# Two layers of a hybrid decoder trunk on one core: sixteen of the twenty-two gate/up tiles of each layer as seven half products, with the weight sums on VectorE

## The chip, the core and the metric

The kernel runs on one core of a Trainium2 chip. The metric is device time in microseconds (us), the median of three runs of the whole program; smaller is better. The core has TensorE (PE in the profile, its weight loads apart as PEld), VectorE (DVE), ScalarE (ACT), GpSimd (POOL) and SyncE (SP), which issues nearly all DMAs here.

## The reference

A trunk of two layers over 512 tokens of width 1024. Each layer mixes tokens (three groups of heads behind one input projection, then an output projection) and then runs a SwiGLU feed-forward of width 2816, each between RMS norms and with a residual. The change is in the feed-forward:

```python
def hybrid_layer(x, ...):
    h = rms_norm(x, pre_mix_norm)
    proj = h @ w_in
    ...
    mix = jnp.concatenate([y_ssd, y_sb, y_moba], axis=-1) @ w_out
    x = x + rms_norm(mix, post_mix_norm)
    h2 = rms_norm(x, pre_ffn_norm)
    f = (jax.nn.silu(h2 @ w_gate) * (h2 @ w_up)) @ w_down
    return x + rms_norm(f, post_ffn_norm)
```

All tensors are float32. The kernel keeps every matrix product at nearly that precision by splitting both operands into a high and a low part of the type fp32r, which TensorE takes, and adding three products (high by high, high by low, low by high).

## The kernel before

One function, `trunk`, writes the whole program; a scheduler then sets the order of the instructions of each engine from the order in which they are written, from priorities (`tc.high_priority(offset=...)`) and from its own estimate of when operands are ready. Each engine then runs its instructions strictly in that order, and waits on semaphores where an operand or a buffer isn't ready.

Weights come in chunks of 128 partitions by 1024 numbers (512 KB). `chunk` (L120) takes one of three raw buffers `wr`, starts the DMA on SP's queue (L122), and splits the chunk into `wh` and `wl`, four buffers of each: ScalarE rounds into `wh` (`split`, L108), and VectorE subtracts that from the raw chunk into `wl` (L109). A raw buffer is free for the next DMA once L109 has read it; a pair `wh`, `wl` is free once TensorE has used it.

The feed-forward's input `h2` stands transposed (features on partitions, tokens along the free dimension) in two tiles `hT`, the high and the low part, eight blocks of 128 features by 512 tokens. `pre_norm` (L173) makes it, token tile by token tile (four tiles of 128 tokens): normalize (L179), transpose on TensorE into a PSUM bank (`to_fm`, L164), split from the bank into `hT` (`to_hT`, L108 and L109). For token tiles 2 and 3 it has one bank each, so that the second four of eight transposes wait until the first four have been split.

Gate and up (L580 to L590): 22 feature tiles `i`. Each takes a gate chunk and an up chunk and runs 24 matmuls for each of them (8 blocks of features by three passes; `fm_mm`, L206, matmul at L210), every one with a 128x128 stationary block of weights and 512 tokens moving, into a bank of PSUM each. The first two tiles (`CUT = 2`) run as two halves of 256 tokens, so that the first half can start before token tiles 2 and 3 are there. Then `silu` of the gate bank on ScalarE (L147) and the product with the up bank on VectorE (L590) give `GT[i]`. There are four pairs of banks in turn.

Down (L596 to L619): for each `i`, `GT[i]` is split into `gs`, two of eight tiles `R` (L606), and TensorE multiplies it with a down chunk (L599), 24 matmuls of 512 columns into all eight banks. In the mixer the tiles `R` serve the softplus values of one attention and the output projection's left operand; the tiles `F28` to `F39` hold the mixer's outputs and scratch.

The lines that the change and the prediction touch: `to_hT` (L167), `pre_norm` (L173), the tile lists (L66, L67, L82, L226), the gate/up loop (L577 to L590), the row loads of the gains behind it (L592 to L594), and the first splits of the down loop (L606).

## Time and profile before

| | us |
|---|---|
| median of three runs (1266.46 to 1266.77) | 1266.76 |
| the profiled execution's own time | 1262.44 |
| its span, first to last instruction | 1260.6 |
| PE busy in it | 1235.3 |
| DVE busy | 612.5 |
| ACT busy | 498.6 |
| one whole gate/up tile of 512 tokens (48 matmuls), from the trace | 10.88 |

TensorE is busy for 98% of the span, at full clock nearly throughout; VectorE and ScalarE are busy for half of it or less. The gate/up stage is about 283 to 511 us in the first layer and 905 to 1134 us in the second, the down stage about 116 us behind each. A busy share says only how long an instruction occupied its engine; how fast instructions follow each other is read from their start times in the timeline.

### The profile page before, as it was taken

What the parts mean: (1) busy time and instruction counts of PE and PEld (TensorE: products, weight loads), DVE (VectorE), ACT (ScalarE), POOL (GpSimd) and SP (SyncE); (2) the same over time, 40 slices, a digit from 0 to 9 for tenths busy, and PEclk for the clock granted to TensorE, in tenths of its full rate; (3) what the DMA queues carried; (4) which work ended last, traced back from release to release, by engine and by line L of the source; (5) the groups of instructions that cost most, each with busy time, mean ns of one, the idle gap of its engine ahead of it and who ended that gap; (6) DMA issues with size and microseconds to landing.
All of it is one profiled execution on the core that took longest, in us unless ns stands there. A gap on an engine that the chain in (4) does not pass through costs nothing.

```text
span 1260.6 us, 15385 instructions
## 1 busy us (share of the span) xinstructions
PE 1235.3 (98%) x6118; PEld 1037.5 (82%) x6118; DVE 612.5 (49%) x1011; ACT 498.6 (40%) x892; POOL 53.8 (4%) x88
## 2 busy tenths in 40 slices
PE   6999999999999999999999999999999999999997
PEld 5787888898888888888877788888988888888886
DVE  5466857874322222333465577588542222223334
ACT  5556763453222222332355656536432222222332
POOL 1010000100000000000010100001000000000000
PEclk9999999999999999999999999999999999999999
DMA  6332223343233332233333322133242322332321
GB/s 241 118 108 77 85 93 101 109 134 113 89 99 101 100 95 91 100 100 100 101 109 108 134 69 84 60 100 117 93 134 100 98 90 97 101 101 96 90 83 67
DMA packets 40760, 128.70 MB, mean 102 GB/s; under 512 B 5456, under 2 KB 5744, under 8 KB 40688
## 3 DMA queue, kind: packets, MB, share of 16 engines
q1 hardware_dynamic: 39344, 123.49, 30.5%
q0 software_dynamic: 1344, 4.23, 1.0%
q8 instruction: 48, 0.79, 0.3%
q14 instruction: 24, 0.20, 0.0%
HBM read 123.47 MB, written 4.23 MB: 101 GB/s over the span
## 4 chain that ended last, share of the span: by engine, by line
PE 95%; DVE 2%; ACT 1%; issue 1%; DMA 0%; SPq 0%; DVEq 0%; POOLq 0%; POOL 0%; ACTq 0%
PE B L210 52%; PE B L599 18%; PE B L201 7%; PE B L549 7%; PE B L324 2%; PE B L331 1%; PE B L437 1%; PE B L302 1%; PE B L164 1%; PE B L509 1%; PE B L303 1%; PE B L433 1%; PE B L351 1%; PE B L560 0%; PE B L515 0%
## 5 line engine op out<-in xcount | busy, mean ns | idle before, releaser
L210 PE MATMUL B<-hT,wh 128*128 128x512 f32 (+1 forms) x2048 | 609.0, 379 | 2.2 <-ACT F L291 2.2
L210 PEld LDWEIGHTS B<-hT,wh 128*128 128x128 f32 x2048 | 376.1, 189 | 71.6 <-ACT F L291 3.3
L210 PE MATMUL B<-hT,wl 128*128 128x512 f32 (+1 forms) x1024 | 386.6, 378 | 0.0
L109 DVE TENSOR_TENSOR wl<-wr,wh 128x1024 fp32r<-128x1024 f32 x204 | 248.6, 1224 | 254.1 <-ACT wh L108 252.6
L108 ACT ACTIVATE wh<-wr 128x1024 fp32r<-128x1024 f32 x204 | 214.9, 1057 | 391.3 <-PE B L210 314.1
L210 PEld LDWEIGHTS B<-hT,wl 128*128 128x128 f32 x1024 | 193.3, 189 | 33.7
L599 PE MATMUL B<-wh,R 128*128 128x512 f32 x704 | 190.1, 389 | 0.0
L599 PEld LDWEIGHTS B<-wh,R 128*128 128x128 f32 x704 | 132.1, 188 | 27.4
L599 PE MATMUL B<-wl,R 128*128 128x512 f32 x352 | 110.0, 389 | 0.0
L109 DVE TENSOR_TENSOR R<-F,R 128x512 fp32r<-128x512 f32 (+2 forms) x76 | 45.9, 607 | 122.1 <-ACT R L108 121.9
L108 ACT ACTIVATE R<-F 128x512 fp32r<-128x512 f32 (+2 forms) x76 | 42.4, 560 | 144.1 <-PE B L599 139.0
L590 DVE TENSOR_TENSOR F<-B,F 128x512 f32<-128x512 f32 x44 | 30.4, 691 | 127.6 <-PE B L210 127.6
L201 PE MATMUL B<-wh,hT 128*128 128x512 f32 x256 | 82.7, 399 | 2.4 <-DVE hT L109 2.4
L599 PEld LDWEIGHTS B<-wl,R 128*128 128x128 f32 x352 | 66.1, 188 | 13.7
L549 PE MATMUL B<-wh,R 128*128 128x512 f32 x256 | 76.9, 398 | 0.0
L155 POOL TENSOR_TENSOR SM<-SM,mhalf 128x1 f32<-128x1 f32 (+2 forms) x50 | 35.4, 711 | 737.1 <-DVE SM L154 464.5
L201 PEld LDWEIGHTS B<-wh,hT 128*128 128x128 f32 x256 | 48.0, 190 | 12.9 <-DVE hT L109 2.9
L549 PEld LDWEIGHTS B<-wh,R 128*128 128x128 f32 x256 | 47.6, 188 | 9.9 <-DVE R L109 0.4
L201 PE MATMUL B<-wl,hT 128*128 128x512 f32 x128 | 50.5, 394 | 0.0
L143 ACT ACTIVATE F<-F 128x512 f32<-128x512 f32 (+3 forms) x80 | 39.0, 499 | 16.2 <-DVE F L220 15.2
L549 PE MATMUL B<-wl,R 128*128 128x512 f32 x128 | 43.0, 394 | 0.0
L464 DVE SCALAR_TENSOR_TENSOR F<-B,cw,F 128x511 f32<-128x511 f32 (+2 forms) x48 | 35.7, 745 | 10.4 <-ACT F L462 9.9
(147 smaller groups left out, 990.8 us busy)
## 6 DMA issues: line engine op xcount, KB each, us to landing
wr<-in_wch_dram SPq DMA_DIRECT2D x204, 512.0 KB, 3.6
x<-in_x_dram SPq DMA_DIRECT2D x16, 256.0 KB, 3.6
F<-in_gains_dram SPq DMA_DIRECT2D x16, 256.0 KB, 4.7
F<-acd POOLq DMA_DIRECT2D x16, 256.0 KB, 6.2
xsave<-x SPq DMA_DIRECT2D x8, 256.0 KB, 2.1
x<-xsave SPq DMA_DIRECT2D x8, 256.0 KB, 3.4
out_dram<-x SPq DMA_DIRECT2D x8, 256.0 KB, 2.1
F<-in_mixgain_dram SPq DMA_DIRECT2D x4, 256.0 KB, 4.9
```

What stands on the lines that cost most here:

```text
L108: A.activation(hi, src, AF.Copy)
L109: return eng.tensor_tensor(lo, src, hi.bitcast(F32), op=OP.subtract)
L143: order["exp"][group] = A.activation(o, i, f, **kw)
L155: G.tensor_tensor(r, m, mhalf[:, 0:n], op=OP.pow)
L164: T.transpose(p[:, i * P:(i + 1) * P], srcs[q + i], ident)
L201: T.matmul(p, hT[a][:, k, t * P:(t + 1) * P], w[k // 2][b][:, (k % 2) * 512:(k % 2 + 1) * 512], start=n == 0, stop=n == 3 * KT - 1)
L210: T.matmul(p[:, t0 * P:t1 * P], w[b][:, k * P:(k + 1) * P], hT[a][:, k, t0 * P:t1 * P], start=first and n == 0, stop=n == 3 * KT - 1, skip ...
L324: T.matmul(pz[:, o:w], ntri if i2 == i else nones, s2, start=False, stop=i2 == NT - 1 and n == 1, skip_group_check=True)
L464: V.scalar_tensor_tensor(u[:, j:], p[:, :S - j], cw[:, i, 3 - j:4 - j], u[:, j:], op0=OP.mult, op1=OP.add)
L549: T.matmul(OB[j][hf], lt, w[b][:, hf * 512:(hf + 1) * 512], start=k == ks[0] and a == 0 and b == 0, stop=k == ks[-1] and a == 1)
L590: V.tensor_tensor(GT[i], pu, sg, op=OP.mult)
L599: T.matmul(B[2 * t + hf], gs[a][:, t * P:(t + 1) * P], w[b][:, hf * 512:(hf + 1) * 512], start=i == 0 and a == 0 and b == 0, stop=i == HT ...
```

## The change

The gate/up product of a tile is seen as a 2 by 2 block product. Let `A` be the input, cut in token halves (rows) and feature halves (columns), and `B` the gate and up weights of a feature tile, cut in feature halves (rows) with gate and up as its two columns. The eight half products (12 matmuls of 256 columns each, with the three passes) are replaced for 16 of the 22 tiles by seven, in Winograd's form of Strassen's scheme. Tiles 0, 1, 5, 9, 13 and 17 stay as they were (`PLAIN`).

Three things are added for that:

- sums of the input, once in a layer: `pre_norm` also copies the transposed, unsplit input to spare tiles (`keep`, on ScalarE), and VectorE forms four combinations of each feature-half block (eight subtractions or sums of 128x512) and splits them into `XS` (eight more operations of 128x512 on VectorE, eight on ScalarE);
- sums of the weights, for each of the 16 tiles: four sums of 128x512 on VectorE, and the split of them and of two raw blocks: `w0` (gate, 1024), `t24` (two blocks of 512, split apart), `t13` (1024), `b22` (512). One tile takes all four pairs of `wh` and `wl`, and both its raw chunks must be there for the first sum;
- the outputs are put together from four half banks with seven operations of 128x256 on VectorE, one copy and two `silu` of 128x256 on ScalarE.

A tile's matmuls have 256 columns: 84 of them instead of 48 of 512. The eight half banks of two sets take turns. To make room, the tiles `R` become halves of four tiles `RR`, and `F28` to `F39` halves of six tiles `D`; in the gate/up stage `D0` to `D5`, `RR0` and `RR1` hold `XS`, and `RR2` and `RR3` the weight sums. The down stage takes `RR` back.

```diff
+PLAIN = (0, 1, 5, 9, 13, 17)
...
-    def to_hT(t):
+    def to_hT(t, keep=None):
         def dst(q, n, p):
+            if keep is not None:
+                A.activation(keep[q // 4], p, AF.Copy)
             sl = slice(t * P, (t + 1) * P)
             split(p.rearrange("p (k l) -> p k l", k=4), hT[0][:, q:q + n, sl], hT[1][:, q:q + n, sl])
...
+        QA = [[QF[0], F[22]], [QF[1], F[23]], [F[24], F[26]], [F[25], F[27]]]
...
-                    pre_norm(j, grow2, take_jk(), ring(OB[j] if j < 2 else OB[j][0:1]))
+                    pre_norm(j, grow2, take_jk(), ring(OB[j] if j < 2 else OB[j][0:1]), QA[j])
...
+        k4 = "p (k l) -> p k l"
+        XS = [slot(f"D{i}", F32R, D) for i in range(6)] + RR[0:2]
+        XS = [[t.rearrange(k4, k=4) for t in XS[2 * i:2 * i + 2]] for i in range(4)]
+        TT = [slot(f"RR{i}", F32, D) for i in (2, 3)]
+        for c in range(2):
+            (a11, a12), (a21, a22) = QA[c], QA[2 + c]
+            s2, s3 = QF[4 + c], QF[2 + c]
+            V.tensor_tensor(a22, a22, a21, op=OP.subtract)
+            V.tensor_tensor(s2, a11, a22, op=OP.add)
+            V.tensor_tensor(s3, a11, a21, op=OP.subtract)
+            V.tensor_tensor(a12, s2, a12, op=OP.subtract)
+            for n, src in enumerate((a22, s2, s3, a12)):
+                split(src.rearrange(k4, k=4), *[x[:, :, c * P:(c + 1) * P] for x in XS[n]])
...
+        def left(j, a, k):
+            if j < 3:
+                return hT[a][:, k + (4 if j else 0), 256 if j == 2 else 0:512 if j == 2 else 256]
+            return XS[j - 3][a][:, k]
+
+        def product(p, w, half, j, first):
+            for k in range(4):
+                for n, (a, b) in enumerate(PASSES):
+                    T.matmul(p, w[b][:, half * 512 + k * P:half * 512 + (k + 1) * P], left(j, a, k),
+                             start=first and k == 0 and n == 0, stop=k == 3 and n == 2, skip_group_check=True)
+
+        def plain(i):
             wg = chunk(l, C_GU + 2 * i)
             wu = chunk(l, C_GU + 2 * i + 1)
...
+        def seven(i):
+
+            rg, ru = take_raw(), take_raw()
+            b11, b21, b12, b22 = rg[:, lo5], rg[:, hi5], ru[:, lo5], ru[:, hi5]
+            for n, r in enumerate((rg, ru)):
+                nc.sync.dma_start(r, wch[l, C_GU + 2 * i + n])
+            t13, t24 = TT
+            w0, w24, w13, w22 = [(take_hi(), take_lo()) for _ in range(4)]
+            with tc.high_priority(offset=SPLIT_OFF):
+                split(rg, *w0)
+                V.tensor_tensor(t13[:, lo5], b11, b12, op=OP.add)
+                V.tensor_tensor(t24[:, lo5], t13[:, lo5], b22, op=OP.add)
+                split(t24[:, lo5], w24[0][:, lo5], w24[1][:, lo5])
+                V.tensor_tensor(t13[:, hi5], b12, b22, op=OP.add)
+                split(t13, *w13)
+                V.tensor_tensor(t24[:, hi5], t24[:, lo5], b21, op=OP.add)
+                split(t24[:, hi5], w24[0][:, hi5], w24[1][:, hi5])
+                split(b22, w22[0][:, lo5], w22[1][:, lo5])
+            pa, pb, pc, pd = [b[:, 0:256] for b in take_set()]
+            t0, t1 = GT[i][:, 0:256], GT[i][:, 256:512]
+            wv, xv, uv, sg = take_ct(), take_ct(), take_ct(), take_ct()
+            product(pa, w0, 0, 0, True)
+            A.activation(wv, pa, AF.Copy)
+            product(pb, w24, 0, 4, True)
+            V.tensor_tensor(wv, pb, wv, op=OP.subtract)
+            product(pd, w13, 1, 5, True)
+            V.tensor_tensor(xv, wv, pd, op=OP.subtract)
+            product(pc, w13, 0, 3, True)
+            V.tensor_tensor(xv, xv, pc, op=OP.subtract)
+            product(pa, w0, 1, 1, False)
+            silu(sg, pa)
+            product(pd, w24, 1, 2, False)
+            V.tensor_tensor(uv, pd, wv, op=OP.subtract)
+            silu(uv, uv)
+            V.tensor_tensor(t1, xv, uv, op=OP.mult)
+            product(pc, w22, 0, 6, False)
+            V.tensor_tensor(wv, wv, pc, op=OP.subtract)
+            V.tensor_tensor(t0, wv, sg, op=OP.mult)
+
+        for i in range(HT):
+            (plain if i in PLAIN else seven)(i)
+
+        RR = [slot(f"RR{i}", F32R, D) for i in range(4)]
+        R = cut(RR)
```

Outside gate/up, the engines' orders stay as they were but for names, the added copies and a few neighbours among the output projection's last matmuls. Three places where the order moves carry the prediction. Names there are those of the tiles with the program's own numbers behind the underscore; `x4` means four alike in a row; line numbers of the changed kernel are its own (L114 and L115 are `split`, L644 to L649 the weight sums, L656 to L671 the putting together, L632 the product of a plain tile, L598 to L601 the input's sums).

VectorE, the middle of the gate/up stage of the first layer, before: two low parts and one product to a tile.

```order
L109 TENSOR_TENSOR wl0_123<-wr0_116,wh0_119 128x1024
L590 TENSOR_TENSOR F6_1239<-B6_114,F28_81 128x512
L109 TENSOR_TENSOR wl1_124<-wr1_117,wh1_120 128x1024
L109 TENSOR_TENSOR wl2_125<-wr2_118,wh2_121 128x1024
L590 TENSOR_TENSOR F7_1240<-B0_108,F29_82 128x512
```

VectorE, from tile 19's second product to the first weight sum of tile 21, in the change:

```order
L660 TENSOR_TENSOR F2_65<-F2_65,B0_98 128x256
L115 TENSOR_TENSOR wl1_114<-RR3_2163,wh1_110 128x512
L662 TENSOR_TENSOR F2_65<-F2_65,B7_105 128x256
L115 TENSOR_TENSOR wl2_115<-RR2_2162,wh2_111 128x1024
L115 TENSOR_TENSOR wl0_113<-wr1_107,wh0_109 128x1024
L666 TENSOR_TENSOR F3_66<-B0_98,F2_65 128x256
L115 TENSOR_TENSOR wl1_114<-RR3_2163,wh1_110 128x512
L668 TENSOR_TENSOR F9_1232<-F2_65,F3_66 128x256
L670 TENSOR_TENSOR F2_65<-F2_65,B7_105 128x256
L671 TENSOR_TENSOR F9_1232<-F2_65,F3_66 128x256
L115 TENSOR_TENSOR wl3_116<-wr2_108,wh3_112 128x512
L644 TENSOR_TENSOR RR2_2162<-wr0_106,wr1_107 128x512
```

The next tile's low parts now stand between the operations on this tile's banks, and the next but one tile's sum behind them; that sum reads the raw buffer `wr1` that the fifth row here frees.

VectorE, where token tiles 2 and 3 of the first layer come into `hT`, before:

```order
L179 SCALAR_TENSOR_TENSOR F43_96<-x30_1253,SM_127,F20_73 128x512
L179 SCALAR_TENSOR_TENSOR F44_97<-x31_1254,SM_127,F21_74 128x512
L109 TENSOR_TENSOR hT1_107<-B1_109,hT0_106 128x4x128
L109 TENSOR_TENSOR hT1_107<-B3_111,hT0_106 128x4x128
L109 TENSOR_TENSOR hT1_107<-B1_109,hT0_106 128x4x128
L109 TENSOR_TENSOR hT1_107<-B3_111,hT0_106 128x4x128
L109 TENSOR_TENSOR wl0_123<-wr1_117,wh0_119 128x1024
```

and in the change:

```order
L649 TENSOR_TENSOR RR3_2163<-RR3_2163,wr1_107 128x512
L187 SCALAR_TENSOR_TENSOR F43_84<-x30_1243,SM_117,F20_73 128x512
L187 SCALAR_TENSOR_TENSOR F44_85<-x31_1244,SM_117,F21_74 128x512
L600 TENSOR_TENSOR F6_1229<-F4_1227,F24_77 128x512
L115 TENSOR_TENSOR hT1_97<-B1_99,hT0_96 128x4x128
L600 TENSOR_TENSOR F7_1230<-F5_1228,F25_78 128x512
L115 TENSOR_TENSOR hT1_97<-B3_101,hT0_96 128x4x128
L115 TENSOR_TENSOR D5_2161<-F6_1229,D4_2160 128x4x128
L115 TENSOR_TENSOR D5_2161<-F7_1230,D4_2160 128x4x128
L598 TENSOR_TENSOR F26_79<-F26_79,F24_77 128x512
L115 TENSOR_TENSOR hT1_97<-B1_99,hT0_96 128x4x128
```

The input's sums and their splits stand among the splits into `hT`, on which TensorE's second halves of tiles 0 and 1 wait.

ScalarE, the end of gate/up in the first layer, before:

```order
L108 ACTIVATE wh2_121<-wr1_117 128x1024
L147 ACTIVATE F29_82<-B7_115 128x512
L138 ACT_TABLE_LOAD
L143 ACTIVATE SM_127<-smal_4354 128x8
L108 ACTIVATE wh3_122<-wr2_118 128x1024
```

and in the change (`F12` is `GT[0]`):

```order
L114 ACTIVATE wh1_110<-wr0_106 128x1024
L153 ACTIVATE F3_66<-F3_66 128x256
L144 ACT_TABLE_LOAD
L114 ACTIVATE RR0_4380<-F12_67 128x512
L114 ACTIVATE RR1_4381<-F13_68 128x512
L149 ACTIVATE SM_117<-smal_5258 128x8
```

Before, the splits of `GT[0]` to `GT[3]` stood far earlier, behind those tiles' products; now `GT[0]`'s, which the first down matmul reads, stands behind the last tile's `silu` and the load of a table, and its target `RR0` was read by the last tile's seventh product.

## Rows read from the trace of the kernel before

**Rows 1.** The page: span, busy time of each engine, shares of the chain.

```profile
span 1260.6 us, 15385 instructions
PE 1235.3 (98%) x6118; PEld 1037.5 (82%) x6118; DVE 612.5 (49%) x1011; ACT 498.6 (40%) x892; POOL 53.8 (4%) x88
PE 95%; DVE 2%; ACT 1%; issue 1%; DMA 0%; SPq 0%; DVEq 0%; POOLq 0%; POOL 0%; ACTq 0%
```

**Rows 2.** The chain in order of time: start us, length us, what.

```profile
268.59 10.67 PE B L210 x89
283.32 228.17 PE B L210 x1048
```

**Rows 3.** PE's timeline in tile 0: start us, busy us, line, operation, shape, count.

```profile
268.66 0.40 PE L210 MATMUL B<-hT,wh 128*128 128x256 f32 x2
...
269.02 0.40 PE L210 MATMUL B<-hT,wh 128*128 128x256 f32 x2
```

**Rows 4.** Timeline of one gate/up tile, other engines: in brackets idle before, releaser.

```profile
484.33 1.06 ACT L108 ACTIVATE wh<-wr 128x1024 fp32r<-128x1024 f32 x1 [4.38 <-PE B L210]
...
485.42 1.23 DVE L109 TENSOR_TENSOR wl<-wr,wh 128x1024 fp32r<-128x1024 f32 x1 [4.21 <-ACT wh L108]
...
486.68 5.77 SPq L122 DMA_DIRECT2D wr<-in_wch_dram  x2
...
495.21 1.06 ACT L108 ACTIVATE wh<-wr 128x1024 fp32r<-128x1024 f32 x1 [4.38 <-PE B L210]
```

**Rows 5.** Groups by shape: count | busy us, mean ns of one | idle before.

```profile
L210 PE MATMUL B<-hT,wh 128*128 128x256 f32 x256 | 47.4, 285 | 0.0
L210 PEld LDWEIGHTS B<-hT,wh 128*128 128x128 f32 x2048 | 376.1, 189 | 71.6 <-ACT F L291 3.3
L109 DVE TENSOR_TENSOR wl<-wr,wh 128x1024 fp32r<-128x1024 f32 x204 | 248.6, 1224 | 254.1 <-ACT wh L108 252.6
L109 DVE TENSOR_TENSOR R<-F,R 128x512 fp32r<-128x512 f32 x52 | 36.0, 692 | 119.4 <-ACT R L108 119.4
L501 DVE TENSOR_TENSOR F<-B,cst 128x256 f32<-128x256 f32 x8 | 3.4, 420 | 7.6 <-PE B L499 7.6
L435 ACT ACTIVATE F<-B 128x256 f32<-128x256 f32 x8 | 3.0, 379 | 2.0 <-PE B L433 2.0
```

**Rows 6.** DVE's timeline where its operations stand back to back.

```profile
219.13 0.68 DVE L518 TENSOR_TENSOR F<-F,F 128x512 f32<-128x512 f32 x1
219.85 0.69 DVE L529 TENSOR_TENSOR F<-F,F 128x512 f32<-128x512 f32 x1
...
221.41 0.42 DVE L501 TENSOR_TENSOR F<-B,cst 128x256 f32<-128x256 f32 x1
221.75 0.68 DVE L517 TENSOR_TENSOR F<-B,SM 128x512 f32<-128x512 f32 x1
...
230.14 3.49 DVE L109 TENSOR_TENSOR wl<-wr,wh 128x1024 fp32r<-128x1024 f32 x3
233.54 0.68 DVE L511 TENSOR_TENSOR F<-B,F 128x512 f32<-128x512 f32 x1
234.14 0.68 DVE L517 TENSOR_TENSOR F<-B,SM 128x512 f32<-128x512 f32 x1
```

**Rows 7.** The page's DMA issues: count, size, median us from issue to landing.

```profile
wr<-in_wch_dram SPq DMA_DIRECT2D x204, 512.0 KB, 3.6
```

**Rows 8.** PE's and DVE's timeline where token tiles 2 and 3 arrive.

```profile
279.10 0.60 PE L164 MATMUL B<-ident,F 128*128 128x128 f32 x4
...
280.38 1.39 PE L164 MATMUL B<-ident,F 128*128 128x128 f32 x8
...
280.37 0.69 DVE L109 TENSOR_TENSOR hT<-B,hT 128x512 fp32r<-128x512 f32 x1 [1.14 <-ACT hT L108]
```

**Rows 9.** From gate/up to down: ACT's and PE's timeline.

```profile
507.65 1.28 ACT L138 ACT_TABLE_LOAD   x1
...
511.33 0.39 PE L599 MATMUL B<-wh,R 128*128 128x512 f32 x1
```

More of the change, by code (lines that the diff above doesn't have):

```diff
@@ L64, in trunk, with slot, cut @@
     dr = ctx.enter_context(tc.tile_pool(name="dr", bufs=1, space=DRAM))
-    F = [None if 4 <= i < 12 or 18 <= i < 20 else cp.tile([P, 512], F32, name=f"F{i}") for i in range(NF)]
-    R = [cp.tile([P, 512], F32R, name=f"R{i}") for i in range(8)]
+    def slot(name, dt=F32, n=512):
+        return cp.tile([P, n], dt, name=name, bufs=1)
+    def cut(tiles):
+        return [t[:, h * 512:(h + 1) * 512] for t in tiles for h in range(2)]
+    F = [None if 4 <= i < 12 or 18 <= i < 20 or 28 <= i < 40 else cp.tile([P, 512], F32, name=f"F{i}")
+         for i in range(NF)]
+    DD = [slot(f"D{i}", F32, D) for i in range(6)]
+    RR = [slot(f"RR{i}", F32R, D) for i in range(4)]
     hT = [cp.tile([P, KT, 512], F32R, name=f"hT{a}") for a in range(2)]
@@ L80, in sm @@
         return SM[:, used[0] - n:used[0]]
-    def slot(name, dt=F32):
-        return cp.tile([P, 512], dt, name=name, bufs=1)
     def ring(items):
@@ L171, in to_hT, with pre_norm @@
         return dst
-    def pre_norm(t, grow, jk, bank):
+    def pre_norm(t, grow, jk, bank, keep=None):
         ssp = sm(2)
@@ L179, in pre_norm @@
             V.scalar_tensor_tensor(jk[hf], xres[t][hf], r[:, 0:1], grow[hf], op0=OP.mult, op1=OP.mult)
-        to_fm([jk[i // 4][:, (i % 4) * P:(i % 4 + 1) * P] for i in range(KT)], to_hT(t), bank)
+        to_fm([jk[i // 4][:, (i % 4) * P:(i % 4 + 1) * P] for i in range(KT)], to_hT(t, keep), bank)
     def post_norm(t, banks, grow, jk, store=None):
@@ L225, in trunk @@
     VT, LM = F[0:4], F[20:28]
-    MIXA, MG = F[28:32], F[32:34]
     QNAMES = [f"F{i}" for i in range(4, 12)] + [f"x{t}{h}" for t in range(NT) for h in range(2)] + ["F18", "F19"]
@@ L260, in trunk @@
     for l in range(DEPTH):
+        if l > 0:
+            DD = [slot(f"D{i}", F32, D) for i in range(6)]
+        F[28:40] = cut(DD)
+        R = cut(RR)
+        MIXA, MG = F[28:32], F[32:34]
         tok_proj(l, C_V, ring([B[0], B[2], B[4], B[6]]), lambda t, p: A.activation(VT[t], p, AF.Copy),
@@ L590, in trunk @@
             V.tensor_tensor(GT[i], pu, sg, op=OP.mult)
-        grow3 = load_row(gains[l, 3], F[34:36])
+        def seven(i):
[35 more added lines that the diff above has]
+            V.tensor_tensor(t0, wv, sg, op=OP.mult)
@@ L593, in trunk @@
+        for i in range(HT):
+            (plain if i in PLAIN else seven)(i)
+        RR = [slot(f"RR{i}", F32R, D) for i in range(4)]
+        R = cut(RR)
+        grow3 = load_row(gains[l, 3], F[41:43])
         if l + 1 < DEPTH:
-            grow4 = load_row(gains[l + 1, 0], F[36:38])
+            grow4 = load_row(gains[l + 1, 0], F[20:22])
         def down(i, t, w, gs, halves=(0, 1)):
```

6 lines of the change are left out of this document (4 added, 2 removed).

## The prediction

> **What bounds the kernel now.** I read the page first: TensorE is busy for 1235.3 of 1260.6 us and holds 95% of the chain that ends last, VectorE is busy for 49% and ScalarE for 40% [rows 1]. So the time is a sum of matmuls, and an edit counts for what it does to the rate at which matmuls follow each other and to the gaps between them. The chain in order of time shows where the change acts: from 283 to 511 us the first layer's gate/up runs as one unbroken piece of matmuls; the second layer has a piece of the same length [rows 2]. There is nothing to win there but fewer or shorter matmuls, and every wait that the change brings is a loss.
>
> Busy time misleads on the rate, since matmuls overlap: a 256-column matmul shows 285 ns [rows 5]. Start times are what counts. In tile 0, which already runs in halves of 256 columns, 89 matmuls take 10.67 us, 0.120 us each [rows 2], and three take 0.36 us [rows 3]; every one has new weights. A whole tile with 512 columns takes 495.21 - 484.33 = 10.88 us from ScalarE's first split of one tile to that of the next [rows 4], TensorE never idle [rows 2]: 0.227 us for each of 48. Halving the columns takes off 0.107 us; 0.013 us of each matmul is fixed.
>
> **The gain on TensorE.** A seven-product tile has 84 x 0.120 = 10.08 us of matmuls in place of 10.88. That is 0.80 us, not the 1.36 us that an eighth of the work would be, since the fixed part is paid 84 times instead of 48. Sixteen tiles in two layers: 32 x 0.80 = 25.6 us off. This is the only gain; the DMA traffic stays at two chunks a tile, and TensorE's order elsewhere hardly moves.
>
> Here a rule of the Trainium skill speaks against the change: in "TensorE: Matmul & The Clock Gate", the section on the mechanism of packing small matmuls says that a weight load overlaps a running matmul only where the row groups differ, and the section on LDWEIGHTS gives a load of 128 columns about 107 ns (its columns over 1.2 GHz). By the two, more loads would cost in full. The trace doesn't agree (a load is shown as 189 ns, and yet 0.120 us pass from start to start); I come back to it as a rival.
>
> **What VectorE has to do.** A plain tile costs it two low parts of 1024 and one product of 512. A seven-product tile costs two operations of 1024 (low parts of `w0` and `t13`), seven of 512 (four sums, three low parts) and seven of 128x256 (putting together). Their price has two ends. By the means of rows [rows 5] it is 2 x 1.224 + 7 x 0.692 + 7 x 0.420 = 10.23 us, more than TensorE's 10.08. But back to back they follow faster: 3.40 us for three of 1024 (1.13 each), 0.60 for 512, 0.34 for 256; one that reads its predecessor's result took 0.72 in place of 0.60 [rows 6]. That gives 2 x 1.13 + 7 x 0.60 + 7 x 0.34 = 8.84 us, and some 0.3 for dependent ones: 9.1 us, 91% of the tile. I take 9.1, since these rows show the same operations in a queue. ScalarE has four to five us to a tile and isn't near its limit.
>
> A busy queue can still hold TensorE up, because VectorE works in order and the buffers are few. The tightest loop goes through the raw buffers: the next tile's up chunk goes where this tile's gate chunk was, so its DMA starts when `w0`'s low part is made. A DMA starts at once then (485.42 + 1.23 = 486.65, issued at 486.68 [rows 4]) and lands after 3.6 us [rows 7]. Then VectorE has, by its order, the four weight sums and `t24`'s first low part (512 each), among them three operations on banks (256 each), and the low parts of `t13` and `w0` (1024 each), 3.00 + 1.02 + 2.26 = 6.28 us back to back. The loop is 9.88 us, just under 10.08; by means it is 3.46 + 1.26 + 2.45 + 3.6 = 10.77. I followed the order through such a tile by hand, with the durations of rows: `w24`'s first low part is there about 1 us before TensorE wants it, `t13`'s and `w0`'s more than 2 us before. After a plain tile, which asks VectorE for less than 3 us out of 10.88, the lead is made up. So in the steady stretches I count no wait; it costs 0 to 15 us (below).
>
> **What is paid at the ends of the stage, in each layer.** (1) Token tiles 2 and 3: today the second four transposes wait for the bank to be split; they start at 280.38 and VectorE's split at 280.37 [rows 8]. The copy to `keep` goes ahead of each split on ScalarE (0.5 us), and a sum of the input stands ahead of the split on VectorE (0.6 us), while the matmuls that TensorE had in between now stand ahead of the first transposes. That is a gap of about 1.6 us; today part of that is lost too (eight transposes take 1.39 us there, four 0.60). By my walk tile 1 ends 0.8 us later than today (0 to 2.5, if the eight sums and eight splits of the input hold up later ones as well). By my walk through the order `XS` is complete 2 us before the first product that reads it, covered by the second halves of tiles 0 and 1. (2) In tile 2, and only there, the order has the fifth product right behind the first, in the same bank, which ScalarE must have copied between: 0.285 - 0.120 = 0.17 us until the last matmul is through, a copy of 128x256 at 0.38 us [rows 5], and 0.1 us to start again, 0.65 us. (3) Down: today its first matmul follows the last one of gate/up with no gap, 511.33 [rows 9], because `GT[0]` was split long before. Now the split's target is what the last seventh product reads, so ScalarE can start it only after the last matmul: 0.17 + 0.6 us. In the first layer the load of a table, 1.28 us [rows 9], stands ahead of it and behind a weight split and the last `silu`; there I get 2.0 us, in the second layer, where no table is loaded, 0.8 us. VectorE's half of that split is wanted 3.6 us later (16 matmuls need the high part alone) and costs nothing.
>
> **The sum.** -25.6 + 2 x (0.8 + 0.65) + 2.0 + 0.8 = -19.9 us. On the profiled execution, 1262.44 us (span 1260.6), that makes 1242.5; the median of the runs, 1266.76, stands 4.3 us above it and the same difference gives 1246.9, say 1247 us.
>
> **The rivals.** *The ends are hidden.* If the gaps of (1) to (3) fall on time that TensorE loses today, only 25.6 us count: 1241 us. For it: the transposes lose some time today already [rows 8]. Against: nothing can hide (3).
>
> *VectorE is the bound, mildly.* If its operations, broken up by waits, cost their means rather than their distance, the raw-buffer loop is 10.77 us, and each seven-product tile that follows another (11 of 16 in a layer: two in each of four groups of three, three in the last group of four) loses 0.69 us: +15.2, that is 1262 us. For it: 91% leaves little; against: the lead of 1 to 2 us absorbs half of it in a group of three, giving about 1255.
>
> The Trainium skill's "VectorE: DVE Perf Modes" has a rule for this end, in the section on the DRAIN: the next operation starts when the pipeline is empty. By that rule the means would hold; the rows with 0.60 us between starts of operations that show 0.68 don't agree.
>
> *VectorE is the bound, and the change is slower.* Place: the same loop, where `t13`'s and `w0`'s low parts each wait for ScalarE to make the high part, which itself waits for TensorE to free the buffer. If one such high part, 1.06 us [rows 4], is exposed in the loop, it is 11.8 us for 22 tiles: 22 x 1.75 = 38 us, and 1247 + 38 = 1285. It decides from 19.9 / 22 = 0.90 us of lost time in each of these tiles on; below that the change still gains. Against it: in the order, TensorE's first products of the next tile stand between this tile's, which gives these parts time.
>
> *The change doesn't do what it says, because weight loads set the rate.* If a load couldn't overlap, 36 more of them in a tile at 189 ns [rows 5] would cost 6.8 us against 1.3 us for the 3072 columns saved (0.107 us for 256): 5.5 x 32 = +176, some 1440 us. By the load of 107 ns in the Trainium skill's "TensorE: Matmul & The Clock Gate" it would be an estimated 2.6 us a tile and some 1350 us. The distance of 0.120 us [rows 3] excludes it, unless the 256-column matmuls of the `XS` tiles differ from those of `hT`. A milder form, in which TensorE's distance is 0.130 us, gives 10.9 us a tile: no gain, and 1272 us with the ends.
>
> **How the numbers follow.** Forecast 1247, 0.70 (its own range 1243 to 1253); ends hidden, 1241, 0.08; VectorE mildly the bound, 1253 to 1263, 0.12; VectorE the bound and slower, 0.07; rate of weights, 0.03. Below 1240 there is nothing, and above 1259 about half of the mild case and all of the last two, 0.16 in all; the range 1240 to 1259 leaves that out. A measurement of this kernel can tell about 0.2%, 2.5 us, from no change. Faster by more than that: the first two and nearly all of the third, 0.88; within it 0.04; slower 0.08.
>
> **What would show it.** Right: in the profile of the changed kernel the products' line starts a matmul every 0.120 us; a seven-product tile takes 10.1 us, and with plain tiles at 10.9 the stage from tile 2 on is 12.8 us shorter; VectorE is busy for some (3 x 10.2 + 3.1) / 41.1 = 82% of the stage, as its rows show it, in place of 3.1 us in each 10.9; TensorE is never idle before the products but in tile 2; a gap of 2 us ahead of the first down matmul in the first layer and about 0.8 in the second, released by ScalarE's `RR` split; a gap of about 1.6 us at the transposes of token tiles 2 and 3. Wrong: a distance between matmuls above 0.125 us; TensorE idle before the products with VectorE's `wl` as releaser, tile after tile, with more of it late in each group of three; VectorE's sums idle until the raw chunk lands; or a wait for `XS` in tile 2 of several us.

## The result, and the profile after

The changed kernel takes 1249.48 us (median of four runs, 1248.47 to 1250.28) against 1266.61 before: 0.987 of the time, 95% interval 0.9856 to 0.9887 (a fourth run of the kernel before, 1263.45, makes its median 1266.61 here and not 1266.76). That is 17.1 us less, where the sum said 19.9, and inside the range. The profiled execution has 1248.79 us.

The page of the changed kernel, in the lines of [rows 1]:

```profile
span 1247.0 us, 18442 instructions
PE 1214.4 (97%) x7270; PEld 1074.4 (86%) x7270; DVE 825.5 (66%) x1459; ACT 590.3 (47%) x1084; POOL 54.0 (4%) x88
PE 91%; DVE 3%; ACT 2%; issue 1%; DMA 1%; SPq 0%; DVEq 0%; POOLq 0%; POOL 0%; ACTq 0%
```

TensorE still carries the time. VectorE has 213 us more to do (825.5 against 612.5), and its share of the chain grew by one point only.

**The rate.** PE's timeline inside a seven-product tile (start us, busy us, line, shape, count), and the chain's pieces for most of a group of three such tiles and of the last group:

```profile
366.02 0.40 PE L619 MATMUL B<-hT,wh 128*128 128x256 f32 x2
366.26 0.28 PE L619 MATMUL B<-hT,wl 128*128 128x256 f32 x1
366.38 0.40 PE L619 MATMUL B<-hT,wh 128*128 128x256 f32 x2
```

```profile
340.03 29.27 PE B L619 x244
...
463.51 37.45 PE B L619 x312
```

366.38 - 366.02 is three matmuls: 0.120 us each, as in [rows 3]. 29.27 / 244 and 37.45 / 312 are 0.120 too, without a hole: 84 of them are 10.08 us. The step that carries the gain held to the hundredth.

**The waits.** All that TensorE waits for from tile 2 to the down stage of the first layer (engine, line, releaser: us, times, longest):

```profile
PE B L685 <- ACT RR L114: 3.1, 1, 3.1
PE B L619 <- ACT F L656: 0.5, 1, 0.5
```

There is no `wl` among the releasers: VectorE holds nothing up in the steady stretches. The two waits that are there were both named, but the first is longer than the 2.0 us expected (3.29 from one matmul to the next, less the pitch). In the second layer they are 0.8 and 0.5.

**The stage.** I call stage what lies between the first gate/up matmul and the first down matmul. It took 242.90 us in each layer before. It now takes 235.55 (269.96 to 505.51) and 233.14 (886.94 to 1120.08): 17.11 us less in the sum, which is the difference of the medians. Between the two profiles the spans differ by 13.6 only. The other 3.5 us are not from these stages; the chain of after and of before, at a place of the mixer that the change leaves alone:

```profile
101.45 6.16 PE B L218 x19
```

```profile
101.49 4.61 PE B L210 x19
```

The same 19 matmuls take 1.55 us longer; 48 others, from 629.46 us in after and 635.15 in before, take 12.82 us in place of 11.17: 3.2 us of the 3.5. The granted clock says why; the stretch from 101 us in after and in before (window, its length, busy times, PEclk, DMA share, GB/s):

```profile
101.00:110.00 9.00, 8.55 (x38) 7.17 (x39) 3.75 (x9) 4.28 (x12) 0.00 (x0) 0.81 0.19 60
```

```profile
101.00:109.00 8.00, 7.51 (x42) 6.57 (x43) 3.96 (x10) 4.64 (x13) 0.00 (x0) 1.00 0.25 68
```

In the first of them the 512-column matmuls start every 0.43 us in place of 0.23, the lower level of 1.2 GHz, for some three us behind a wait of 0.70 us; in before the same wait, equally long, has no such stretch. So this is luck of the execution, and the stages are what I compare below.

### The profile page after: what moved, and what is told of

The parts are those of the page before. It is cut to its first block, busy times and chain, and to the rows that moved or that the text cites. A ratio compares the mean times of both kernels' runs of the same rounds, so it can differ in the third digit from the quotient of the medians.

```text
span 1247.0 us, 18442 instructions
## 1 busy us (share of the span) xinstructions
PE 1214.4 (97%) x7270; PEld 1074.4 (86%) x7270; DVE 825.5 (66%) x1459; ACT 590.3 (47%) x1084; POOL 54.0 (4%) x88
## 4 chain that ended last, share of the span: by engine, by line
PE 91%; DVE 3%; ACT 2%; issue 1%; DMA 1%; SPq 0%; DVEq 0%; POOLq 0%; POOL 0%; ACTq 0%
PE B L218 24%; PE B L619 23%; PE B L685 19%; PE B L209 7%; PE B L561 7%; PE B L336 2%; PE B L343 1%; PE B L449 1%; PE B L314 1%; DMA wr<-in_wch_dram 1%; PE B L170 1%; PE B L521 1%; PE B L315 1%; DVE wl L115 1%; ACT wh L114 1%
## 5 line engine op out<-in xcount | busy, mean ns | idle before, releaser
L218 PE MATMUL B<-hT,wh 128*128 128x512 f32 (+1 forms) x1024 | 296.6, 370 | 2.2 <-ACT F L303 2.2
L115 DVE TENSOR_TENSOR wl<-wr,wh 128x1024 fp32r<-128x1024 f32 (+1 forms) x204 | 230.5, 1137 | 84.2 <-ACT wh L114 82.2
L114 ACT ACTIVATE wh<-wr 128x1024 fp32r<-128x1024 f32 (+1 forms) x204 | 200.4, 989 | 129.6 <-DMA wr<-in_wch_dram 40.1
L685 PE MATMUL B<-wh,RR 128*128 128x512 f32 x704 | 189.8, 389 | 3.9 <-ACT RR L114 3.9
L218 PE MATMUL B<-hT,wl 128*128 128x512 f32 (+1 forms) x512 | 188.2, 369 | 0.0
L685 PEld LDWEIGHTS B<-wh,RR 128*128 128x128 f32 x704 | 132.0, 188 | 31.6 <-ACT RR L114 4.3
L619 PE MATMUL B<-hT,wh 128*128 128x256 f32 x768 | 152.1, 283 | 0.9 <-ACT F L656 0.9
L619 PE MATMUL B<-D,wh 128*128 128x256 f32 x768 | 148.9, 283 | 0.0
L619 PEld LDWEIGHTS B<-D,wh 128*128 128x128 f32 x768 | 123.9, 192 | 0.4
L114 ACT ACTIVATE wh<-RR 128x512 fp32r<-128x512 f32 (+1 forms) x96 | 73.9, 774 | 97.7 <-PE B L619 42.5
L685 PE MATMUL B<-wl,RR 128*128 128x512 f32 x352 | 109.5, 389 | 0.0
L115 DVE TENSOR_TENSOR RR<-F,RR 128x512 fp32r<-128x512 f32 x48 | 33.1, 691 | 111.3 <-ACT RR L114 110.6
L115 DVE TENSOR_TENSOR wl<-RR,wh 128x512 fp32r<-128x512 f32 (+1 forms) x96 | 82.5, 863 | 17.7 <-ACT wh L114 17.2
L114 ACT ACTIVATE RR<-F 128x512 fp32r<-128x512 f32 x48 | 30.0, 629 | 131.2 <-PE B L685 130.8
L561 PE MATMUL B<-wh,RR 128*128 128x512 f32 x256 | 77.2, 398 | 0.0
```

Source lines behind the costliest of these rows:

```text
L114: A.activation(hi, src, AF.Copy)
L115: return eng.tensor_tensor(lo, src, hi.bitcast(F32), op=OP.subtract)
L218: T.matmul(p[:, t0 * P:t1 * P], w[b][:, k * P:(k + 1) * P], hT[a][:, k, t0 * P:t1 * P], start=first and n == 0, stop=n == 3 * KT - 1, skip ...
L561: T.matmul(OB[j][hf], lt, w[b][:, hf * 512:(hf + 1) * 512], start=k == ks[0] and a == 0 and b == 0, stop=k == ks[-1] and a == 1)
L619: T.matmul(p, w[b][:, half * 512 + k * P:half * 512 + (k + 1) * P], left(j, a, k), start=first and k == 0 and n == 0, stop=k == 3 and n == ...
L685: T.matmul(B[2 * t + hf], gs[a][:, t * P:(t + 1) * P], w[b][:, hf * 512:(hf + 1) * 512], start=i == 0 and a == 0 and b == 0, stop=i == HT ...
```

## The experiments

Times are medians; since executions differ by a few us in the granted clock, the lengths of the two stages in the traces stand beside them (before 242.90 + 242.90 = 485.80, after 468.69).

**1. Another target for down's first split** (`ring2`).

```diff
-            gs = R[(i % 4) * 2:(i % 4) * 2 + 2]
+            gs = R[((i + 2) % 4) * 2:((i + 2) % 4) * 2 + 2]
```

> The down stage's ring of split targets starts two places further, so that GT[0] and GT[1] are split into RR2 and RR3 (read last by the weight splits of tile 21) and not into RR0 and RR1 (read by the last seventh product). Theory (the waits of 3.13 and 0.76 us ahead of the first down matmul come from the target alone): both go but for about 0.5 us in the first layer, where the first down matmul's bank is still read by VectorE; about 3.5 us less than the changed kernel, 1246.0. Rival (the table load and the last silu on ScalarE hold the split up whatever its target): the first layer keeps some 3 us, only the 0.8 of the second goes, 1248.7.

1242.28 us, ratio to before 0.9814 (0.9797 to 0.9832); stages 232.22 + 232.23 = 464.45. No wait ahead of down is left in either layer, not even for the bank: 4.24 us off the stages, that is 3.33 and 0.91, all that the first down matmul was late. The median fell by 7.2; the other 3 us are not from the stages, and two of its five runs had a granted clock of 0.998, where the changed kernel's had 0.993 to 0.995. ScalarE's rows at the end of the stage are the same in both traces: two `RR` splits ahead of the last products (492.54 and 493.85 us here, 491.60 and 492.79 in the changed kernel) and two behind the table load. With the other target the early two are those of `GT[0]` and `GT[1]`. So the target made the wait; the table load only lengthened it where the split stood behind it.

**2. The gain row's load out of the way** (`mg_late`). Looking for why the first layer's wait is 2.4 us longer than the second's, when the table load is 1.28 us, I found a transfer that I had overlooked. SP's queue at the end of the first layer's stage:

```profile
492.45 0.33 SPq L109 DMA_DIRECT2D D<-in_mixgain_dram  x1
492.88 0.37 SPq L128 DMA_DIRECT2D wr<-in_wch_dram  x1
493.30 0.42 SPq L109 DMA_DIRECT2D D<-in_mixgain_dram  x1
495.55 8.57 SPq L128 DMA_DIRECT2D wr<-in_wch_dram  x3
```

The next layer's gain row goes into a tile that now holds sums of the input until tile 21, so it can't be loaded earlier, and it stands between down's first chunks.

```diff
-        nc.sync.dma_start(raw, wch[l, i])
+        order["chunk"] = nc.sync.dma_start(raw, wch[l, i])
...
-        load_row(mixgain[l], MG)
+        with after([order["chunk"]] if l else []):
+            load_row(mixgain[l], MG)
```

> The changed kernel with one thing moved: the load of the second layer's gain row for the mixer (two transfers of 256 KB into a tile that holds sums of the input until tile 21's products) is issued behind the down stage's last weight chunk and not among its first ones. All orders on TensorE, ScalarE and VectorE are as in the changed kernel. Theory (in the first layer the first down chunks land 0.9 us later than in the second because they share the queue and the bandwidth with this load, and ScalarE's queue in front of the split of GT[0] ends that much later): the wait ahead of the first layer's first down matmul falls from 3.13 to about 2.2 us, everything else stays, 0.9 us less in all, which is at the limit of what the times can show and plain in the trace. Rival (the table load alone makes the difference between the layers): 3.1 us stay.

The wait falls from 3.13 to 2.40 us, with the orders of the three engines unchanged:

```profile
503.82 0.73 PE L686 MATMUL B<-wh,RR 128*128 128x512 f32 x2 [2.40 <-ACT RR L114]
```

Stages 234.76 + 233.48 = 468.24; 1249.76 us, ratio 0.9884 (0.9856 to 0.9911), no difference that the times show. Theory said 0.9 us. The second layer, where nothing was moved, shows how far landings differ by themselves: there the high parts ahead of down waited 2.68 us for their chunk in place of 2.36, and the wait of 0.76 us became 1.08. So some 0.7 us of the first layer's term are this transfer, give or take 0.3.

**3. No plain tile behind the first two** (`plain2`).

```diff
-PLAIN = (0, 1, 5, 9, 13, 17)
+PLAIN = (0, 1)
```

> Tiles 5, 9, 13 and 17 too run as seven products: twenty in a row, with no plain tile in which VectorE could make up a lead. Theory (VectorE's work costs the distance of starts, 9.1 us of 10.08, and the raw-buffer loop 9.88): no wait, 8 more tiles at 0.79 us, 1249.5 - 6.3 = 1243.2. Rival (means of rows: the loop takes 10.77 us): each of the tiles loses up to 0.69 us once the lead is used up, some 36 tiles, up to +25 - 6.3: 1260 to 1268. Between them, a loop of 10.2 would give 1247.

1240.10 us, ratio 0.9798 (0.9778 to 0.9818); stages 230.93 + 229.64 = 460.57, 8.12 less than after: 1.6 from shorter waits ahead of down and 6.5 from eight tiles, where theory said 6.3. The chain of the first layer is one piece from tile 2 on:

```profile
298.42 186.02 PE B L619 x1546
```

186.02 / 1546 = 0.120 us. With nothing to recover in, VectorE still delays no gate/up product by more than 0.1 us: the rival by which its operations cost their means has fallen. What is left ahead of the first layer's down, 1.65 us, does end with VectorE: its operation on the bank that the first down matmul fills (L666, at 498.47) stands behind two low parts whose high parts had waited 3.90 us for a chunk.

**4. All tiles plain, the sums of the input still made** (`allplain`).

```diff
-PLAIN = (0, 1, 5, 9, 13, 17)
+PLAIN = tuple(range(22))
```

> All 22 tiles plain, everything else as changed: the copies, the input's sums and their splits are made, and used nowhere. Theory (the sums cost TensorE only the gap at the transposes, 1.3 us more than before in each layer, and the wait ahead of down goes with the last seventh product): 2.5 us more than the kernel before, 1269. Rival (the new tiles and the copies cost nothing and the gap belongs to the seven-product tiles): as before, 1266.6. Other rival (the eight sums and eight splits hold up later work on VectorE): 1271 or more.

1267.14 us, ratio 1.0018 (1.0004 to 1.0033); stages 243.72 + 243.71 = 487.43, 0.82 us a layer more than before, without any product saved: more than the first rival's nothing, and less than the 1.3 of the theory. PE's timeline at the transposes of token tiles 2 and 3:

```profile
281.39 0.60 PE L170 MATMUL B<-ident,F 128*128 128x128 f32 x4
281.75 0.48 PE L218 MATMUL B<-hT,wh 128*128 128x256 f32 x2
...
282.31 0.60 PE L170 MATMUL B<-ident,F 128*128 128x128 f32 x4
284.01 0.65 PE L170 MATMUL B<-ident,F 128*128 128x128 f32 x4 [1.10 <-DVE hT L115]
```

The copies and sums alone make a gap of 1.10 us. Here four matmuls stand between the first two groups of transposes; in the changed kernel they stand ahead of both, and its gap is 1.58: four times 0.120 more.

**5. Halves without the scheme** (`halves22`), from the kernel before.

```diff
-CUT = 2
+CUT = 22
```

> The kernel before with all 22 plain tiles in two halves of 256 tokens: the same products with 96 matmuls of 256 columns in place of 48 of 512, and no seven-product tile. Theory (a matmul has a fixed part of 0.013 us: 96 x 0.120 = 11.52 us for a tile in place of 10.88): 40 x 0.64 = 25.6 us more than before, 1292. Rival (halving the columns costs nothing, and the eighth of the work that the change saves is lost elsewhere): 1266.6. Rival (the weight loads of 256-column matmuls show once they go on for long): over 1300.

1288.26 us, ratio 1.0181 (1.0165 to 1.0196); stages 255.67 + 255.68. 12.77 us more a layer over 20 tiles is 0.64 us a tile, as expected to the hundredth: 96 matmuls at 0.120 are 11.52 us. (The medians differ by 22.1 us and not by 25.5; all runs here had a granted clock of 0.997, most of those of before 0.994.) So halving the columns costs 0.64, dropping the eighth half product gives back 12 x 0.120 = 1.44, and the 0.80 between them is the change.

**6. The copy behind the split** (`keepafter`).

```diff
-            if keep is not None:
-                A.activation(keep[q // 4], p, AF.Copy)
             sl = slice(t * P, (t + 1) * P)
             split(p.rearrange("p (k l) -> p k l", k=4), hT[0][:, q:q + n, sl], hT[1][:, q:q + n, sl])
+            if keep is not None:
+                A.activation(keep[q // 4], p, AF.Copy)
```

> The copy of the transposed input to its spare tile stands behind the split into hT and not ahead of it. Theory (the gap of 1.58 us at the transposes of token tiles 2 and 3 is the copy of 0.5 us and the input's sum of 0.6 us ahead of the split, in each layer): the gap shrinks to about 0.5 us, 2 us less in all, 1247.5. Rival (the gap is the bank itself: two transposes share a bank, and the copy also has to be through before the bank is free, whichever comes first): the gap stays at 1 to 1.6 us, 1249 to 1249.5. A third way: the sums get so late that the first product with a sum of the input waits: 1250 or more.

1250.37 us, ratio 0.9878 (0.9864 to 0.9892): no gain; stages 236.37 + 234.06 = 470.43. TensorE's waits from 262 us to the down stage:

```profile
PE B L685 <- ACT RR L114: 3.2, 1, 3.2
PE B L619 <- DVE wl L115: 1.2, 1, 1.2
PE B L218 <- ACT hT L114: 0.7, 1, 0.7
PE B L619 <- ACT F L656: 0.2, 1, 0.2
```

The wait of 1.58 us at the transposes became one of 0.7, and one of 1.2 us for a weight split took its place: VectorE's order moved with the copies, and the stages are 1.74 us longer than the changed kernel's. That is the third way, but through a weight sum and not through a sum of the input.

**7. Both edits of 1 and 3** (`both`).

> The two edits together: twenty seven-product tiles in a row, and the down stage's ring of split targets two places further. From the traces: the ring alone takes 3.9 us off the stage to the first down matmul (3.17 + 0.74), four more seven-product tiles in each layer 8 x 0.79 = 6.3. Theory (the two don't touch each other): the stage is 10.2 us shorter than in the changed kernel, no wait ahead of down, about 1239.5 at the clock at which the changed kernel has 1249.5. Rival (down's first split now waits for VectorE, which has no plain tile ahead of it): a wait of 1 us or more ahead of down stays in each layer, 1241.5 or more.

1238.48 us, ratio 0.9788 (0.9773 to 0.9802): 28 us less than before and 11 less than the change, the fastest median here. Stages 229.79 + 228.87 = 458.66, 10.03 less than after, where theory said 10.2. Ahead of down 0.22 us are left in the first layer, for a chunk's high part, and nothing in the second.

The loop through the raw buffers can be read in this trace. VectorE's first sum of a tile (L644) waits for its chunk, and from there to the end of `w0`'s low part, which frees a buffer for the next DMA, its operations follow without idle time (L666 is the one behind that low part); the third line is the chain's:

```profile
473.57 0.69 DVE L644 TENSOR_TENSOR RR<-wr,wr 128x512 f32<-128x512 f32 x1 [0.98 <-DMA wr<-in_wch_dram]
...
479.85 0.42 DVE L666 TENSOR_TENSOR F<-B,F 128x256 f32<-128x256 f32 x1
...
479.96 3.60 DMA wr<-in_wch_dram
...
483.66 0.69 DVE L644 TENSOR_TENSOR RR<-wr,wr 128x512 f32<-128x512 f32 x1 [0.99 <-DMA wr<-in_wch_dram]
```

VectorE's part is 479.85 - 473.57 = 6.28 us and the landing 3.60, both as predicted; but 0.1 us pass from the low part to the transfer and 0.1 from the landing to the sum. The loop is 10.09 us here and 9.9 to 10.1 in most tiles of the first layer, not 9.88: beside TensorE's 10.08 it has nothing to spare. Where a chunk took 4.41 us to land (378.63), the loop took 10.89, and at 386 us TensorE lost 0.5 us, nearly all of it to VectorE's operation on a bank (L660).

**8. How near is VectorE?** (`both_dup1`, `both_dup2`) In `both`, the first weight sum once or twice more in every seven-product tile:

```diff
                 V.tensor_tensor(t13[:, lo5], b11, b12, op=OP.add)
+                V.tensor_tensor(t13[:, lo5], b11, b12, op=OP.add)
```

> The kernel with both edits and, in every seven-product tile, the first weight sum (512 columns, 0.60 us from start to start) made a second time; nothing else. It asks how near VectorE is to being the bound where no plain tile follows. Theory A (the sum of its work decides: 9.1 + 0.6 = 9.7 us of 10.08): no wait, the same time as without it, 1239.5. Theory B (the loop through the raw buffers decides: 9.88 + 0.6 = 10.48 us): 0.4 us for each of some 38 tiles, 15 us more. Theory C (the means of rows: the loop is 10.77 already): ruled out by the run with twenty in a row, which had no such wait.

> As the last one, with the first weight sum made three times: 1.2 us more for VectorE in every seven-product tile. Theory A (the sum of the work): 10.3 us to a tile, 0.2 over TensorE's 10.08, 38 x 0.2 = 8 us more than without. Theory B (the loop through the raw buffers): 11.08 us, 38 us more.

1266.61 us with one and 1262.34 with two: neither theory's number, since less work cost more. What moved is the order. With one, VectorE's rows in a tile (in brackets idle time before and releaser; L644 and L645 are the sum and its repeat, L672 is the last operation of the tile before, and `w0`'s low part ends where the row at 449.65 starts):

```profile
442.43 0.69 DVE L644 TENSOR_TENSOR RR<-wr,wr 128x512 f32<-128x512 f32 x1 [0.35 <-DMA wr<-in_wch_dram]
...
443.64 0.42 DVE L672 TENSOR_TENSOR F<-F,F 128x256 f32<-128x256 f32 x1
...
444.58 0.68 DVE L645 TENSOR_TENSOR RR<-wr,wr 128x512 f32<-128x512 f32 x1
...
449.65 0.69 DVE L115 TENSOR_TENSOR wl<-RR,wh 128x512 fp32r<-128x512 f32 x1
...
453.43 0.69 DVE L644 TENSOR_TENSOR RR<-wr,wr 128x512 f32<-128x512 f32 x1 [0.35 <-DMA wr<-in_wch_dram]
```

VectorE's part of the loop through the raw buffers is 449.65 - 442.43 = 7.22 us, again without idle time, in place of 6.28: the repeat, 0.60, and L672, 0.34, which in `both` stands outside the loop. So the loop is 11.00 us here, and 10.9 us is what a tile takes in the second layer (11.05 in the first, from starts of L667 from 306.24 to 483.06, 16 tiles with a stretch at the lower clock among them). TensorE waits for `wh` in 17 tiles of each layer. This is theory B's loop, with 10.05 in place of 9.88 to start from and one operation more: the extra 0.6 us cost 0.9 us a tile by its place. With two, the products into the same bank stood behind each other in every tile, as in tile 2 of the change, and TensorE waited 0.47 us for the copy in each (18 times in the first layer), a tile taking 10.80 us. That prices term (2) again, 0.7 us, and says nothing on VectorE.

**9. The same with that order held** (`both_ord`, `both_ord_dup1`, `both_ord_dup2`).

```diff
-            product(pc, w13, 0, 3, True)
+            p3 = product(pc, w13, 0, 3, True)
...
-            product(pa, w0, 1, 1, False)
+            with after([p3]):
+                product(pa, w0, 1, 1, False)
```

> The kernel with both edits, and the product that follows in the first product's bank (the second into pa) held behind the fourth product (the first into pc) in every tile, on TensorE's queue alone. Theory (in tile 2 TensorE waits 0.47 us for ScalarE's copy of the bank, 0.74 us from one matmul to the next and back to the pitch, because those two products stand behind each other there and in no other tile): the wait goes in both layers, 1.5 us less than with both edits alone. Rival (the products moved ahead of it in tile 2 need weight sums that VectorE hasn't split by then): a wait for wl in its place, no gain or a loss.

> The last kernel with the first weight sum of every seven-product tile made twice, 0.60 us more for VectorE. Without the order held, this cost 28 us, with TensorE waiting for ScalarE's high parts; the extra sum had moved the order on all engines. Theory A (that order, with t13's second sum behind other work on VectorE, was the cause, and VectorE's 9.0 + 0.6 = 9.6 us fit into 10.08): 0 to 3 us more than the last kernel. Theory B (the loop through the raw buffers, lengthened by the sum, is the cause in whatever order): 15 to 28 us more.

> As the last one with the sum made three times, 1.20 us more for VectorE. Without the order held this cost 23 us, with TensorE waiting 0.47 us in each tile for ScalarE's copy of a bank, since the two products into pa stood behind each other in all of them. Theory (that order was the cause; now VectorE's 9.0 + 1.2 = 10.2 us is the bound, 0.15 over TensorE's 10.08): some 6 us more than with the order held and no extra sum. Rival (VectorE or the loop behind it was the bound, and the wait for the copy only stood in its place): 20 us or more again, now with a wait for wl or wh.

`both_ord`: 1239.17 us (ratio 0.9807, 0.9788 to 0.9825) against 1238.48 (0.9788); the kernel before differs by 3.6 us between the two comparisons, so the stages count: 461.65 against 458.66. The wait for the copy is gone, and waits for `wh` came, 1.6 us in the first layer and 0.8 in the second. That is a loss, as the rival had it, but not by the rival's mechanism: it stands in later tiles, for high parts, behind chunks that landed late. The chain, and the matmul that waits (another such chunk, 5.21 us from 379.62, goes ahead of the wait at 387.59):

```profile
411.48 5.25 DMA wr<-in_wch_dram
...
419.50 0.39 PE L619 MATMUL B<-D,wh 128*128 128x256 f32 x1 [0.99 <-ACT wh L114]
```

With nothing to spare in the loop, a landing of 5.2 us in place of 3.6 reaches TensorE; why these two were slow is open. `both_ord_dup1`: 1271.21, 32 us more and beyond both theories, and 11.19 us a tile in the first layer, 10.9 to 11.0 in the second. Holding TensorE's order didn't hold VectorE's: the repeat stands as far back as it did (412.69 us, where `t13` is whole at 411.8), so this run repeats `both_dup1`, longer loop and all, and whether 9.6 us of work would fit into 10.08 in another order stays open. `both_ord_dup2`: 1249.29, 10.41 us a tile, 10 us more in all than `both_ord` where theory said 6. Here is the bound asked for; the stretch from 300 to 490 us in `both` and in `both_ord_dup2`:

```profile
300.00:490.00 190.00, 189.37 (x1574) 188.81 (x1574) 169.91 (x301) 93.77 (x151) 0.00 (x0) 1.00 0.32 102
```

```profile
300.00:490.00 190.00, 188.37 (x1533) 184.66 (x1531) 186.17 (x330) 83.41 (x144) 0.00 (x0) 1.00 0.32 101
```

In `both`, where every tile has seven products, VectorE is busy for 169.91 / 190 = 89% of 10.08 us: 9.0 us a tile, against 9.1 by my count. Two more sums make it 98% of 10.41, 10.2 us, and with that VectorE is full and sets the pace: in 36 of the 40 tiles a product's weight load waits for VectorE's operation on its bank (L663), 10.6 us in all, and no first sum of a tile in the stretch waits for a chunk. By the means of [rows 5] it would be 10.23 + 2 x 0.692 = 11.6 us. The Trainium skill's "VectorE: DVE Perf Modes", section on the DRAIN, says that the next operation doesn't start until the pipe is empty, but that one that isn't held starts earlier; a queue with two per cent of idle time, which does 11.6 us of rows in 10.41, agrees with the second alone.

## Why the prediction was right, and where it was off

Term by term, in us (a minus is time won); "measured" is from starts of matmuls in the traces of before and after, layer 1 and layer 2.

| term | predicted | layer 1 | layer 2 |
|---|---|---|---|
| 20 tiles from tile 2 on, per layer | -12.8 | -12.67 | -12.72 |
| (1) transposes of token tiles 2 and 3 | +0.8 | +1.29 | +1.29 |
| (2) the copy between two products, tile 2 | +0.65 | +0.74 | +0.74 |
| (3) first down matmul | +2.0 / +0.8 | +3.29 | +0.92 |
| sum | -9.35 / -10.55 | -7.35 | -9.77 |

**The gain on TensorE: right, and for the reason given.** Start times, not busy times, gave the pitch; `halves22` shows the fixed part by itself. The Trainium skill's load of 107 ns that doesn't overlap ("TensorE: Matmul & The Clock Gate") would have cost an estimated 5 us a tile in `halves22`, with 48 more loads; it was 0.64 us.

**VectorE: right in its work, and without the margin I gave its loop.** Its price by distance of starts was 9.1 us and is 9.0; `plain2` excluded the mild rival, and in `both_ord_dup2` 1.2 us more made VectorE the bound. The raw-buffer loop is about 10.05 us in `both` and not 9.88, since I had left out two hand-overs of 0.1 us. That twenty such tiles in a row cost nothing is partly luck: 0.1 us more in the loop would have been over TensorE's 10.08. `both_dup1` shows the loop deciding, in an order that lengthens it.

**(1) was too small by 0.5 a layer.** The gap is the one foretold, 1.58 us for 1.6. But it adds 1.29 to the stage and not 0.8, so only 0.3 us were lost there before; `allplain` gives the same (1.10 less 0.82). I had taken the 1.39 us that eight transposes show as busy, against 0.60 for four, for time that TensorE loses; a busy time isn't a rate, as I had said myself of the matmuls. PE's, ScalarE's and VectorE's timeline of after, where [rows 8] have before:

```profile
281.47 1.04 PE L170 MATMUL B<-ident,F 128*128 128x128 f32 x8
284.08 0.66 PE L170 MATMUL B<-ident,F 128*128 128x128 f32 x4 [1.58 <-DVE hT L115]
...
282.11 0.60 ACT L176 ACTIVATE F<-B 128x512 f32<-128x512 f32 x1 [3.77 <-PE B L170]
282.60 0.59 ACT L114 ACTIVATE hT<-B 128x512 fp32r<-128x512 f32 x1
...
282.74 0.69 DVE L600 TENSOR_TENSOR F<-F,F 128x512 f32<-128x512 f32 x1 [0.65 <-ACT F L176]
283.35 0.68 DVE L115 TENSOR_TENSOR hT<-B,hT 128x512 fp32r<-128x512 f32 x1
```

The chain through the gap is as I had it: transposes, ScalarE's copy (L176), its split (L114), on VectorE a sum (L600) ahead of the low part (L115), then the next transposes.

**(2) was right** to 0.1 us:

```profile
299.52 0.28 PE L619 MATMUL B<-hT,wh 128*128 128x256 f32 x1
300.28 0.38 PE L619 MATMUL B<-hT,wh 128*128 128x256 f32 x1 [0.47 <-ACT F L656]
```

**(3) was the step that failed, in the first layer**: 3.3 us in place of 2.0. ScalarE's and PE's timeline of after, where [rows 9] have before:

```profile
502.16 1.05 ACT L114 ACTIVATE wh<-wr 128x1024 fp32r<-128x1024 f32 x1
503.11 0.41 ACT L153 ACTIVATE F<-F 128x256 f32<-128x256 f32 x1
503.53 1.28 ACT L144 ACT_TABLE_LOAD   x1
504.82 1.15 ACT L114 ACTIVATE RR<-F 128x512 fp32r<-128x512 f32 x2
...
502.10 0.28 PE L619 MATMUL B<-RR,wh 128*128 128x256 f32 x1
505.51 0.73 PE L685 MATMUL B<-wh,RR 128*128 128x512 f32 x2 [3.13 <-ACT RR L114]
```

The queue is the one I had read: weight split, `silu`, table load, split of `GT[0]`. But I had the weight split done when the last matmul ran, and it began only then, because its chunk landed late: two high parts ahead of it waited 3.30 us for DMA. In the second layer the same split began 0.89 us before the last matmul (1118.15 and 1119.04). `mg_late` shows 0.73 us of that as the load of the gain row, a transfer that the change moves by taking its target tile. I had written that the DMA traffic stays at two chunks a tile and had looked at the number of transfers, not at when the new owners of `F28` to `F39` let them start. The other 0.56 us stay in `mg_late`; its last product, and the `silu` behind the weight split:

```profile
501.15 0.28 PE L620 MATMUL B<-RR,wh 128*128 128x256 f32 x1
...
501.42 0.41 ACT L153 ACTIVATE F<-F 128x256 f32<-128x256 f32 x1
```

There the weight split is through 0.27 us behind the start of that last matmul, about when I had it; but the `silu` then takes 0.42 us to the start of the table load. I had named it, and the recorded 2.0 us are hardly more than 0.17 + 0.6 + 1.28, so the sum has nothing for it. The Trainium skill has more for a table load than its row ("ScalarE: Activation LUTs", what ACT_TABLE_LOAD costs: 1.28 us and 1.38 us of draining). By that the term would be an estimated 3.4 us and look right; but the split starts at 504.82, 1.29 us behind the load's start, and the load at the end of the `silu`: no such time shows here.

**The rest of the profile.** I compared with the profiled execution of before, which had one stretch at the lower clock where the profile of after has three. The medians, 1266.6 and 1249.5, differ by what the stages differ.

## What to carry to other kernels

A product saved by Strassen's scheme is worth its matmuls at the pitch of the smaller shape, not a share of the work: here 12 x 0.120 us less 0.64 for halving, 0.80 of 10.88. Count a queue's load by the distance of starts, and count plain tiles in as reserve only if that distance asks for it; here it didn't, and they cost 6.5 us. In a loop that goes through a transfer, count the hand-overs too: two of 0.1 us took all that the loop here had to spare. Whenever a tile gets a second owner, ask of each of its old users, transfers too, when it may now start: the change's two avoidable losses, 4.2 us ahead of the down stage, were both of this kind, and a ring that starts at another tile took them away.

## What was unexpected

Two executions of one kernel can differ by 4 us through stretches of some three us at the lower clock, behind waits of TensorE that in other executions have no such effect: the runs of the kernel before gave 1265.9 to 1267.2 us at a mean granted clock of 0.994 and 1260.7 to 1262.7 at 0.998. With edits of some us, the stage in the trace tells more than a median of three. And an operation added to a scheduled kernel isn't a clean load: 0.6 us of VectorE's time cost 0.9 us a tile by its place, twice as much cost less, and only one run had the same order on three engines as the kernel that it stands beside (`mg_late`), and even there a chunk of the other layer landed 0.3 us later.
